# A decoder layer on one core: norm rows spread over the partitions by a store and a broadcast load instead of TensorE products, and the first head pair's key copies ahead of its value loads

## The chip, the core and the metric

The kernel runs on one core of a Trainium2 chip. The metric is the time of one execution in microseconds (us), smaller is better. Engines: PE (TensorE, matrix products), DVE (VectorE), ACT (ScalarE), POOL (GpSimd) and SP (SyncE, which here only issues DMAs). Each engine has its own instruction queue and works through it in order. A DMA is issued from an engine's queue; if what it moves isn't ready, the queue stands still at it, and everything behind it waits too.

## What is computed

One layer with 1024 tokens and 1024 features, all in float32. Cut to what matters here:

```python
def rmsnorm(x, g):
    return x * lax.rsqrt(jnp.mean(x * x, axis=-1, keepdims=True) + 1e-6) * g

h = x
h = h + 0.5 * rmsnorm(swiglu(rmsnorm(h, ffn1_pre_g), ...), ffn1_post_g)
h = h + rmsnorm(hybrid_mixer(rmsnorm(h, mix_pre_g), ...), mix_post_g)
h = h + rmsnorm(memory_cross_attention(rmsnorm(h, xa_pre_g), rmsnorm(mem, mem_g), ...), xa_post_g)
h = h + 0.5 * rmsnorm(swiglu(rmsnorm(h, ffn2_pre_g), ...), ffn2_post_g)
```

`hybrid_mixer` projects its input once, runs 16 heads of stick-breaking attention on one part and a state-space scan (SSD) on the other, norms the attention's output (1024 features) and the scan's (two groups of 512), and multiplies both by `w_out`. `mem` holds 256 tokens. So every stage begins and ends with a norm: one number for each token, by which all features of the token are multiplied.

## The kernel before

**Layout.** Activations lie transposed: a tile has 128 features on its partitions and 512 tokens along it, eight tiles make the 1024 features, and the tokens are done in two halves, called `hh` 0 and 1. Every operand of a large product is split into a high and a low part, and three matmuls stand for one (`mm3`): high by high, high by low, low by high. The weights are split on ACT (`whi`) and DVE (`wlo`) as they arrive, or earlier, and then written to DRAM ready split (`dwhi`, `dwlo`).

**A norm** takes two steps. `rms_cols` (L322) takes a tile in which the squares of all features have been added up, and multiplies each block of 128 tokens by ones on PE: this gives a column `c` with one partition for each token of a block and one column for each block (128 x 4 for a half, 128 x 8 for both, 128 x 2 for the memory). ACT takes the root and DVE the reciprocal. But the tiles to be scaled have the tokens along the row, and need the number of each token on all 128 partitions. This is what `rms_rows` (L346) makes: for each block PE multiplies the column, broadcast, by the identity into the PSUM tile `ms`, of which there is one, and ACT copies the 512 numbers into the row tile `r`. DVE then multiplies tiles by `r`. The columns are called `cpost` and `cpre` (behind and ahead of a stage), `cy` (the scan's two groups), `cmem` (the memory) and `ca` (the attention's output), and the rows `rpost`, `rpre`, `rm`, `mix_r` and `rn`. In all `rms_rows` is called 20 times.

**The stages**, by when they run in the profiled execution: the first feed-forward block's up-projection to about 545 us and down-projection to 658; the scan to 1010; the attention to 1541; the output projection to 1685; the cross-attention to 1928; the second feed-forward block to the end.

**What sets the order.** PE's order is the program's, but with pieces pinned: the kernel keeps a clock of the PE time that it has issued (`self.clock`, in ns), and `pinned(at)` puts a PE instruction where the clock says so. `self.later` holds steps with due times on the same clock (`post` fills it: columns, rows, then one tile after the other is scaled). `merge` runs two generators so that their PE time advances in a given proportion; the attention of pair `p` runs beside the projection of pair `p + 1`. On the other engines and in the DMA queues a scheduler orders what the program order leaves open.

**The attention's projection** (`inproj(p)`, L1655) makes queries, keys and values of two heads. `kevac` scales the keys by the norm row, splits them and copies them to their places with four DMAs from SP (L1700). The values are differenced, stored to DRAM (`vt`, L1727) and loaded back rearranged with four DMAs (`dv<-vt`, L1731), and `vtr` splits these. For pair 0 nothing runs beside the projection but its own steps. **The output projection** (`mix_out`) first adds up products over the scan's tiles, and then those over the attention's tiles in the PSUM tiles `dn`, of which there are four; each is scaled by the row `rn` made from `ca` as soon as `ca` is known, and only then is its place free.

Of the kernel before, what the change touches and what calls it, by code (L numbers as in the profile page):

```python
# [10 lines left out]
F32 = mybir.dt.float32  # L11
# [7 lines left out]
P = 128  # L19
# [6 lines left out]
MIXED = 6  # L26
# [21 lines left out]
class Kern:  # L48
# [270 lines left out]
                return e.value  # L319


    def rms_cols(self, groups, c, ones=None, r2=None):  # L322


        nc = self.nc
        ps = self.t(self.msp, [P, H], F32, "ms", bufs=1)
        nb = 0
        for g, accs in enumerate(groups):
            w = ones[g] if isinstance(ones, list) else self.ones if ones is None else ones
            for b in range(accs[0].shape[1] // P):  # L330
                for i, acc in enumerate(accs):
                    self.mm(
                        ps[:, nb : nb + 1], acc[:, b * P : (b + 1) * P], w, i == 0, i == len(accs) - 1
                    )
                nb += 1
        if r2 is not None:
            self.kp(nc.vector.tensor_tensor(out=c, in0=ps[:, 0:nb], in1=r2, op=ALU.mult))
            self.kp(nc.vector.tensor_tensor(out=c, in0=c, in1=r2, op=ALU.mult))
            self.kp(nc.scalar.activation(c, c, AF.Sqrt, bias=self.eps))
        else:  # L340
            self.kp(nc.scalar.activation(c, ps[:, 0:nb], AF.Sqrt, bias=self.eps))
        self.kp(nc.vector.reciprocal(c, c))
        if r2 is not None:
            self.kp(nc.vector.tensor_tensor(out=c, in0=c, in1=r2, op=ALU.mult))

    def rms_rows(self, c, r, behind=None):  # L346

# [35 lines left out]

        self.later += [(self.clock + start + step * d, lambda d=d: one(d)) for d in range(KT)]

    def post(self, hh, gname, r2, gnext=None, out=None, step=None, spread=True, pins=(23000, 28000), accs=None, at=None, tail=None, hold=False, late=None):


        nc = self.nc
        t1, t2 = 2500, 6000  # L390
        if accs is None:
            accs = self.new_accs()
# [2 lines left out]
        c = self.t(self.tp, [P, 4], F32, "cpost", bufs=2)  # L395
        r = self.t(self.fp, [P, H], F32, "rpost", bufs=1)

        def cols():
            self.rms_cols([accs], c, r2=r2)

        def rows():
            self.rms_rows(c, r)

        def apply(d):
            F = self.F[hh][d]
# [24 lines left out]
        accs2 = []  # L430
# [35 lines left out]
        if out is None:  # L466
            t -= 300
            c2 = self.t(self.rp, [P, 4], F32, f"cpre{hh}", bufs=2)
            r2_ = self.t(self.rp, [P, H], F32, f"rpre{hh}", bufs=1) if spread else None
            t1, t2 = tail or (t1 + 4000, t2 + 4000)  # L470
            self.held = [lambda: self.rms_cols([accs2], c2)]
# [9 lines left out]
        self.run_later(float("inf"))  # L481
        self.R[hh], self.C[hh] = self.next_norm

    def pre(self, hh, accs, t1, t2):
        c = self.t(self.rp, [P, 4], F32, f"cpre{hh}", bufs=2)
        r = self.t(self.rp, [P, H], F32, f"rpre{hh}", bufs=1)
        with self.pinned(t1):
            self.rms_cols([accs], c)
        with self.pinned(t2):
            self.rms_rows(c[:, :], r)  # L490
        self.R[hh], self.C[hh] = r, c


# [485 lines left out]
    def down1(self, sp, wdn, act_d, xs_d, gpost, gnext):  # L979

        place = self.blocks_down(sp)
        H_ = [[self.t(self.xp, [P, H], F32, f"xh{hh}{d}") for d in range(KT)] for hh in range(2)]
        L_ = [[self.xl(hh, F32) for d in range(KT)] for hh in range(2)]
        stay = {(1, 1): H_[0][4:8] + L_[0][4:8] + H_[0][0:3], (0, 0): H_[1][4:8] + L_[1][4:8] + H_[1][0:3]}
        accs = []

        def squares(hh, d, tag):
            if d == 0:
                accs[:] = self.new_accs(tag)
            self.sumsq(accs, d, self.F[hh][d])  # L990

        def at(t, f, *args):
            self.later.append((self.clock + t, lambda: f(*args)))

        def finish(m, i):
            if m == 3:
                self.run_later(float("inf"))
                for d in range(4):
                    at(5000 + 4000 * d, squares, 0, d, "acc0")
                self.resid(0, 3500, 16000)  # L1000
            elif m == 4:
                self.run_later(float("inf"))
# [247 lines left out]
    def ssd(self, close):  # L1250

        nc, ap = self.nc, self.ap
        with self.tc.tile_pool(name=self.nm("ssa"), bufs=1, reuse_waits="tile") as ep, \
# [269 lines left out]
                            nc.vector.tensor_tensor(out=yacc[hh], in0=yacc[hh], in1=sq, op=ALU.add)  # L1523

            def group_norm(gr):
                c = self.norm_c[gr] = self.t(self.rp, [P, 8], F32, f"cy{gr}")
                self.rms_cols([[y] for y in yacc], c, ones=self.ones512)
# [20 lines left out]
            def keys(n0, n1):  # L1548

                mh, ml, acc, rm = env["mem"]  # L1550
                if n0 == 0:
                    self.mem_c = self.t(self.rp, [P, 2], F32, "cmem")
                    self.rms_cols([[acc]], self.mem_c)
# [93 lines left out]
    def attention(self):  # L1647
        nc, ap = self.nc, self.ap
        with self.pools("at", ["o", "a"], ["w"]) as (op, sp, wsp, pp):
# [52 lines left out]
            def inproj(p):  # L1702
# [12 lines left out]
                def steps(hh, t, before):  # L1715
# [14 lines left out]
                    for q in range(4):  # L1730
                        nc.sync.dma_start(  # L1731
                            out=v[32 * q : 32 * q + 32, :].rearrange("e (j c d) -> e j c d", j=4, c=4), in_=rows[q]
                        )
                    return v

                def vtr(hh, t):

# [41 lines left out]
                for n in range(6):  # L1779
# [24 lines left out]

            def mix_row(i):
                self.mix_r.append(self.t(self.rp, [P, H], F32, f"rpre{i}", bufs=1))
                return self.rms_rows(self.norm_c[i][:, 0:4], self.mix_r[i], tr_tile)

            def scores(p, a, c):

# [106 lines left out]
            def memory_values(mh, ml):  # L1917

                rm = self.t(self.tp, [P, H], F32, "sq1")[:, 0:MEM]
                self.rms_rows(self.mem_c[:, :], rm)  # L1920
                yield
                for n in range(8):
                    w = ready.pop() if ready else next(Wm)
# [26 lines left out]
                yield from drain(0)  # L1950

            def beside():
                late.append(mix_row(1))
                self.first = self.mix_first(ready.pop())
                for n in range(4 * MIXED):
                    if n < 2:
                        for k in ((5, 6), (7,))[n]:
                            mix_split(k)
                    if n == 2:
                        late.pop()()  # L1960
# [10 lines left out]
            self.Wo, self.mix_r, ready, late = self.wstream(wo[0:MIXED]), [], [], []  # L1971
# [38 lines left out]
    def mix_out(self):  # L2010
# [3 lines left out]
        with self.pools("mo", ["r", "a"], ["b"]) as (rp, sp, sp2, dnp):  # L2014
# [53 lines left out]
            for n, (hh, part) in enumerate(passes):  # L2068
# [1 line left out]
                    continue  # L2070
                X = acts.pop(n)
                def norms(t):
                    c = self.norm_c[2] = self.t(self.rp, [P, 4], F32, "ca", bufs=2)
                    with self.pinned(self.clock + t):
                        self.rms_cols([asum[-1:]], c)
                    R[2] = norm_row(2, 0, t + 4000)

                if n == 1:
# [395 lines left out]
```

## Time and profile before

| | |
|---|---|
| time, median of 3 | 2585.72 us (2585.55 to 2587.47) |
| the profiled execution, its own time | 2583.27 us |
| its span | 2581.5 us |
| mean granted clock of PE | 0.999 |

By stages, from the profile's view by windows (us; the stages' limits are rounded):

| stage | from - to | PE busy | DVE busy | ACT busy | DMA share |
|---|---|---|---|---|---|
| feed-forward 1, up | 0 - 545 | 540.99 | 455.85 | 269.10 | 0.72 |
| feed-forward 1, down | 545 - 658 | 111.69 | 94.47 | 59.84 | 0.58 |
| scan | 658 - 1010 | 351.02 | 276.84 | 198.00 | 0.52 |
| attention | 1010 - 1541 | 526.49 | 406.85 | 295.40 | 0.64 |
| output projection | 1541 - 1685 | 144.00 | 110.70 | 63.70 | 0.60 |
| cross-attention | 1685 - 1928 | 242.98 | 157.86 | 136.16 | 0.62 |
| feed-forward 2 | 1928 - 2581.5 | 646.87 | 498.09 | 266.82 | 0.51 |

How to read the profile: a row of a timeline gives the start and the duration in us, the engine (SPq is SP's queue, which issues DMAs), the line of the kernel, the operation, output <- inputs and shape, and in brackets how long the engine was idle just before and what ended the idle time. `x4` at the end says that four like instructions are taken together. Matmuls overlap: what one costs is the distance between starts, not its duration. The view of waits says for PE which operation waited how long (total, times, longest) and for what. The view of DMAs gives for each kind the count, the KB of one and the median time from issue to landing.

### The profile page before, as it was taken

How to read it: one execution, taken by the hardware profiler on the slowest of the kernel's cores; microseconds unless marked ns; L12 is line 12 of the kernel's file. 1: busy time of each engine (PE TensorE's matmuls, PEld its weight loads, DVE VectorE, ACT ScalarE, POOL GpSimd, SP SyncE). 2: the span in 40 equal slices, each digit the busy share in tenths (PEclk: the TensorE clock that was granted, in tenths of full speed). 3: DMA queues.
4: the chain of work that ended last, by engine and by line, in shares of the span. 5: the costliest groups of instructions: out<-in, count | busy, mean ns of one | idle time of the engine just before them, and what ended most of it. 6: DMA issues, size and time to landing. Idle time of an engine off the chain costs nothing. (4 is left out here: it accounts for less than half of the span.)

```text
span 2581.5 us, 36855 instructions
## 1 busy us (share of the span) xinstructions
PE 2564.0 (99%) x12786; PEld 2141.0 (83%) x12786; DVE 2000.7 (78%) x3074; ACT 1289.0 (50%) x2302; POOL 576.5 (22%) x674
## 2 busy tenths in 40 slices
PE   9999999999999999999999999999999999999999
PEld 7888888888787778888888898888888888888887
DVE  7988997779689884787787876876656887777777
ACT  7434444555356663555555654455554433334453
POOL 2555553001000001111111110111012655541000
PEclk9999999999999999999999999999999999999999
DMA  6458988655665516666666655547658443327654
GB/s 240 163 180 293 308 290 305 220 185 166 232 205 197 184 72 212 186 177 160 176 171 152 206 167 202 197 155 260 202 185 304 150 162 111 110 82 237 192 175 147
DMA packets 251628, 498.24 MB, mean 193 GB/s; under 512 B 60592, under 2 KB 69168, under 8 KB 251440
## 3 DMA queue, kind: packets, MB, share of 16 engines
q1 hardware_dynamic: 204176, 387.31, 46.4%
q0 software_dynamic: 23360, 65.03, 8.6%
q10 hardware_dynamic: 23904, 43.53, 4.6%
q8 instruction: 101, 1.65, 0.3%
q14 instruction: 87, 0.71, 0.1%
HBM read 331.65 MB, written 143.13 MB: 184 GB/s over the span
## 5 line engine op out<-in xcount | busy, mean ns | idle before, releaser
L139 PE MATMUL mm<-xh,whi 128*128 128x512 f32 x1312 | 516.7, 403 | 1.1 <-DVE ft L668 0.5
L139 PE MATMUL mm<-xh,wlo 128*128 128x512 f32 x1280 | 491.7, 392 | 0.0
L139 PE MATMUL mm<-xl,whi 128*128 128x512 f32 (+1 forms) x1248 | 485.7, 389 | 0.3 <-DVE xl L277 0.3
L139 PEld LDWEIGHTS mm<-xh,wlo 128*128 128x128 f32 x1280 | 240.6, 188 | 52.4 <-DVE wlo L270 0.5
L139 PEld LDWEIGHTS mm<-xh,whi 128*128 128x128 f32 x1312 | 247.0, 188 | 43.1 <-issue 3.9
L139 PEld LDWEIGHTS mm<-xl,whi 128*128 128x128 f32 x1248 | 235.6, 189 | 33.4 <-DVE xl L277 0.8
L1829 DVE TENSOR_TENSOR_SCAN nb<-nb,begin 128x128 f32<-128x128 f32 (+7 forms) x128 | 172.1, 1347 | 32.3 <-ACT nb L1825 31.9
L1825 ACT ACTIVATE nb<-z,scale 128x128 f32<-128x128 f32 (+2 forms) x192 | 109.5, 580 | 89.5 <-PE z L139 88.6
L270 DVE TENSOR_TENSOR wlo<-wraw,whi 128x1024 fp32r<-128x1024 f32 x61 | 74.6, 1223 | 51.3 <-ACT whi L268 50.9
L268 ACT CAST whi<-wraw 128x1024 fp32r<-128x1024 f32 (+1 forms) x77 | 73.9, 959 | 70.4 <-PE mm L139 43.5
L1846 POOL DMA_DIRECT2D mix<-sq x64 | 53.0, 828 | 248.7 <-DVE sq L1844 181.5
L669 ACT ACTIVATE ft<-ft 128x512 f32<-128x512 f32 x88 | 55.5, 632 | 95.5 <-DVE ft L668 94.9
L139 PE MATMUL dn<-xh,wlo 128*128 128x512 f32 x296 | 101.2, 390 | 0.0
L772 POOL TENSOR_TENSOR wc<-raw,wraw 128x512 f32<-128x512 f32 x55 | 80.7, 1467 | 56.4 <-DVE wlo L270 23.4
L268 ACT CAST ath<-tr 128x512 fp32r<-128x512 f32 (+1 forms) x106 | 57.3, 540 | 66.9 <-PE tr L142 61.9
L772 POOL TENSOR_TENSOR wc<-wraw,raw 128x512 f32<-128x512 f32 x56 | 78.9, 1409 | 52.5 <-DVE whi L270 16.5
L871 POOL TENSOR_TENSOR ft<-ft,e 128x512 f32<-128x512 f32 x37 | 59.7, 1614 | 126.3 <-DVE e L867 51.1
L270 DVE TENSOR_TENSOR atl<-tr,ath 128x512 fp32r<-128x512 f32 (+1 forms) x106 | 66.1, 625 | 28.0 <-ACT ath L268 26.9
L139 PE MATMUL mm<-ath,v 128*128 128x256 f32 x320 | 87.8, 297 | 0.0
L139 PE MATMUL dn<-xh,blk 128*128 128x512 f32 x264 | 85.2, 389 | 0.0
L268 ACT CAST wlo<-wc 128x512 fp32r<-128x512 f32 x79 | 49.1, 621 | 69.2 <-PE dn L139 25.4
L139 PE MATMUL mm<-atl,v 128*128 128x256 f32 x320 | 83.1, 282 | 0.0
(601 smaller groups left out, 6795.2 us busy)
## 6 DMA issues: line engine op xcount, KB each, us to landing
whi<-dwhi SPq DMA_DIRECT2D x82, 512.0 KB, 4.1
wlo<-dwlo SPq DMA_DIRECT2D x82, 512.0 KB, 5.4
wraw<-in_w_gu SPq DMA_DIRECT2D x43, 512.0 KB, 4.0
dwhi<-bh SPq DMA_DIRECT2D x78, 256.0 KB, 4.2
dwlo<-bl SPq DMA_DIRECT2D x78, 256.0 KB, 4.2
raw<-in_w_gu SPq DMA_DIRECT2D x37, 512.0 KB, 4.1
wraw<-xs SPq DMA_DIRECT2D x56, 256.0 KB, 2.9
xs<-ft ACTq DMA_DIRECT2D x54, 256.0 KB, 3.0
```

The source lines that it names most:

```text
L139: self._pe(self.nc.tensor.matmul(out, lhsT, rhs, start=start, stop=stop, skip_group_check=self.more), cost)
L268: self.kp(self.nc.scalar.copy(hi, src))
L270: self.nc.vector.tensor_tensor(out=lo, in0=src, in1=hi.bitcast(F32), op=ALU.subtract)
L669: nc.scalar.activation(t, t, AF.Silu)
L772: inst = (nc.vector if early else nc.gpsimd).tensor_tensor(out=t, in0=a, in1=b, op=op)
L871: nc.gpsimd.tensor_tensor(out=t1, in0=t1, in1=e, op=ALU.mult)
L1825: nc.scalar.activation(nb[:, s0:s1], z[:, 0:n], AF.Sigmoid, scale=sc[:, i : i + 1])
L1829: nc.vector.tensor_tensor_scan(out=nb[:, 0:Wd][:, ::-1], data0=nb[:, 0:Wd][:, ::-1], data1=begin[:, S - Wd : S][:, ::-1], initial=0.0, op0 ...
L1846: nc.gpsimd.dma_start(out=self.mix_d[p][a * 64 : a * 64 + 64, csl], in_=o, accum_op=ALU.add)
```

## The change

`rms_cols` stores the finished column to DRAM, token by token in a row (`norm`), from SP's queue. The new function `row` loads that row back into all 128 partitions of the row tile with one broadcasting DMA, also from SP. 16 of the 20 calls of `rms_rows` become `row`. The four that stay on PE are the two that make the first rows of the kernel, the one behind the first feed-forward block's second half (`pe=True`), and the `cpre` row between the cross-attention and the second feed-forward block's second half. The columns `cy` and `cmem` are stored once and loaded several times.

In the attention the row `mix_r` is loaded earlier than it was computed. In pair 0, for the second half only, the four `dv<-vt` loads are issued behind the keys' copies, and `vtr` follows them.

```diff
-    def rms_cols(self, groups, c, ones=None, r2=None):
+    def rms_cols(self, groups, c, ones=None, r2=None, keep=True):
...
+        if keep:
+            kept = self.tc.dram_tile([nb, P], F32, name=self.nm("norm"))
+            nc.sync.dma_start(out=kept.rearrange("b p -> p b"), in_=c)
+            return kept
+
+    def row(self, kept, r):
+        self.nc.sync.dma_start(out=r, in_=kept.rearrange("b p -> (b p)").partition_broadcast(P))
...
 in post:
         def rows():
-            self.rms_rows(c, r)
+            if pe:
+                self.rms_rows(c, r)
+            else:
+                self.row(kept[0], r)
...
-                q.append((t + t2, lambda: self.rms_rows(c2[:, :], r2_)))
+                q.append((t + t2, lambda: self.row(kept[1], r2_)))
...
-        self.post(1, gpost, self.C[1], gnext, step=2000, accs=accs[:], at=(6500, 9000, 10000), tail=(7500, 10500))
+        self.post(1, gpost, self.C[1], gnext, step=2000, accs=accs[:], at=(6500, 9000, 10000), tail=(7500, 10500), pe=True)
...
 in the scan's keys and the attention's memory_values:
-                        self.rms_rows(self.mem_c[:, :], rm)
+                        self.row(self.mem_c, rm)
...
 in the attention's inproj, steps:
+                    def back():
+                        for q in range(4):
+                            nc.sync.dma_start(... in_=rows[q])
+                        return v
+                    return back if hh and p == 0 else back()
...
-                vtr(1, tv[1])
+                if p:
+                    vtr(1, tv[1])
                 kevac(evac((yield from last), 1), h1)
+                if p == 0:
+                    vtr(1, tv[1]())
...
-                if n == 10:
-                    late.append(mix_row(0))
-                if n == 12:
-                    late.pop()()
+                if n == 8:
+                    mix_row(0)
...
 in mix_out:
-                with self.pinned(self.clock + at):
-                    self.rms_rows(self.norm_c[i][:, 4 * hh : 4 * hh + 4], r)
+                if i < 2:
+                    self.row(self.norm_c[i][4 * hh : 4 * hh + 4], r)
+                else:
+                    with self.pinned(self.clock + at):
+                        self.row(self.norm_c[i], r)
```

**SP, the first pair's second half in the attention.** `vt` is the values' tile in DRAM, `dv` its rearranged copy, `k` the keys of the two heads, `xl` the split keys; `whi` and `wlo` are weights for later products. Before:

```order
L1717 DMA mix_130<-ev_10050 128x512
L1727 DMA vt_10057<-dv_10053 128x512
L182 DMA whi_10117<-dwhi_647 128x1024
L1700 DMA k_9855<-xl_2197_9851 64x512
L1731 DMA dv_10059<-vt_10057 32x16x32 x4
L1700 DMA k_9855<-xl_2198_9852 64x512
L1700 DMA k_9856<-xl_2197_9851 64x512
L1700 DMA k_9856<-xl_2198_9852 64x512
L182 DMA wlo_10118<-dwlo_648 128x1024
```

And in the changed kernel:

```order
L1732 DMA mix_130<-ev_10044 128x512
L1742 DMA vt_10051<-dv_10047 128x512
L182 DMA whi_10111<-dwhi_647 128x1024
L1715 DMA k_9849<-xl_2199_9845 64x512
L1715 DMA k_9849<-xl_2200_9846 64x512
L1715 DMA k_9850<-xl_2199_9845 64x512
L1715 DMA k_9850<-xl_2200_9846 64x512
L1748 DMA dv_10053<-vt_10051 32x16x32 x4
L182 DMA wlo_10112<-dwlo_648 128x1024
```

The four loads of the values' rows stood between the first and the second copy of the keys, and now stand behind the fourth.

**SP, the beginning of the output projection's sums over the attention.** `xl` are activations loaded from `h`, `slo` the scan's tiles, `wraw` weights that are yet to be split. Before:

```order
L382 DMA xl_3532_16186<-h_1270_5772 128x512
L382 DMA xl_3538_16227<-h_1271_5773 128x512
L2041 DMA slo_16256<-mix_138 128x512
L2041 DMA slo_16261<-mix_139 128x512
L185 DMA wraw_16265<-in_w_out 128x1024
L185 DMA wraw_16271<-in_w_out 128x1024
L382 DMA xl_3552_16284<-h_1272_5774 128x512
```

And in the changed kernel, where `norm_16201` is the column `ca` in DRAM and `rn_3536` the row that scales the `dn` tiles:

```order
L352 DMA rn_3591_16499<-norm_9094 128x512
L352 DMA rn_3592_16501<-norm_9796 128x512
L185 DMA wraw_16243<-in_w_out 128x1024
L185 DMA wraw_16249<-in_w_out 128x1024
L185 DMA wraw_16329<-in_w_out 128x1024
L347 DMA norm_16201<-ca_16193 128x4x1
L185 DMA wraw_16335<-in_w_out 128x1024
L352 DMA rn_3536_16203<-norm_16201 128x512
L390 DMA xl_3537_16205<-h_1271_5773 128x512
L2059 DMA slo_16234<-mix_138 128x512
L2059 DMA slo_16239<-mix_139 128x512
```

Four weight loads in a row come ahead of the activations, the column's store stands between the third and the fourth of them, and the row's load directly behind the fourth, ahead of the activations' loads.

**DVE at the same place.** `sq<-dn,rn` is the first `dn` tile scaled by the row. Before:

```order
L342 RECIPROCAL ca_16212<-ca_16212 128x4
L270 TENSOR_TENSOR wlo_16274<-wraw_16271,whi_16273 128x1024
L2007 TENSOR_TENSOR sq_3539_16234<-dn_16177,rn_3536_16220 128x512
L2008 TENSOR_TENSOR xl_3254_14922<-xl_3254_14922,sq_3539_16234 128x512
L2007 TENSOR_TENSOR sq_3540_16250<-dn_16192,rn_3536_16220 128x512
```

In the changed kernel:

```order
L342 RECIPROCAL ca_16193<-ca_16193 128x4
L270 TENSOR_TENSOR wlo_16252<-wraw_16249,whi_16251 128x1024
L270 TENSOR_TENSOR wlo_16332<-wraw_16329,whi_16331 128x1024
L2025 TENSOR_TENSOR sq_3538_16212<-dn_16158,rn_3536_16203 128x512
L2026 TENSOR_TENSOR xl_3255_14912<-xl_3255_14912,sq_3538_16212 128x512
```

A second weight split now stands between the reciprocal and the first scaling.

More of the change, by code (lines that the diff above doesn't have):

```diff
@@ L384, in resid, with post @@
         self.later += [(self.clock + start + step * d, lambda d=d: one(d)) for d in range(KT)]
-    def post(self, hh, gname, r2, gnext=None, out=None, step=None, spread=True, pins=(23000, 28000), accs=None, at=None, tail=None, hold=False, late=None):
+    def post(self, hh, gname, r2, gnext=None, out=None, step=None, spread=True, pins=(23000, 28000), accs=None, at=None, tail=None, hold=False, late=None, pe=False):
         nc = self.nc
@@ L396, in post @@
         r = self.t(self.fp, [P, H], F32, "rpost", bufs=1)
+        kept = []
         def cols():
-            self.rms_cols([accs], c, r2=r2)
+            kept.append(self.rms_cols([accs], c, r2=r2, keep=not pe))
         def rows():
-            self.rms_rows(c, r)
+            if pe:
+                self.rms_rows(c, r)
+            else:
+                self.row(kept[0], r)
         def apply(d):
@@ L470, in post @@
             t1, t2 = tail or (t1 + 4000, t2 + 4000)
-            self.held = [lambda: self.rms_cols([accs2], c2)]
+            self.held = [lambda: kept.append(self.rms_cols([accs2], c2, keep=spread))]
             if not hold:
@@ L482, in flush, with pre @@
         self.R[hh], self.C[hh] = self.next_norm
-    def pre(self, hh, accs, t1, t2):
+    def pre(self, hh, accs, t1, t2, pe=True):
         c = self.t(self.rp, [P, 4], F32, f"cpre{hh}", bufs=2)
@@ L487, in pre @@
         with self.pinned(t1):
-            self.rms_cols([accs], c)
+            kept = self.rms_cols([accs], c, keep=not pe)
         with self.pinned(t2):
-            self.rms_rows(c[:, :], r)
+            if pe:
+                self.rms_rows(c[:, :], r)
+            else:
+                self.row(kept, r)
         self.R[hh], self.C[hh] = r, c
@@ L1525, in group_norm @@
             def group_norm(gr):
-                c = self.norm_c[gr] = self.t(self.rp, [P, 8], F32, f"cy{gr}")
-                self.rms_cols([[y] for y in yacc], c, ones=self.ones512)
+                c = self.t(self.rp, [P, 8], F32, f"cy{gr}")
+                self.norm_c[gr] = self.rms_cols([[y] for y in yacc], c, ones=self.ones512)
             def mem_prep():
@@ L1551, in keys @@
                 if n0 == 0:
-                    self.mem_c = self.t(self.rp, [P, 2], F32, "cmem")
-                    self.rms_cols([[acc]], self.mem_c)
+                    self.mem_c = self.rms_cols([[acc]], self.t(self.rp, [P, 2], F32, "cmem"))
                     yield
@@ L1729, in steps @@
                     rows = o.rearrange("(c e) (j q d) -> q e j c d", c=4, q=4, d=32)
[L1730 to L1734, printed above, removed]
+                    def back():
+                        for q in range(4):
+                            nc.sync.dma_start(
+                                out=v[32 * q : 32 * q + 32, :].rearrange("e (j c d) -> e j c d", j=4, c=4), in_=rows[q]
+                            )
+                        return v
+                    return back if hh and p == 0 else back()
                 def vtr(hh, t):
@@ L1806, in mix_row @@
                 self.mix_r.append(self.t(self.rp, [P, H], F32, f"rpre{i}", bufs=1))
-                return self.rms_rows(self.norm_c[i][:, 0:4], self.mix_r[i], tr_tile)
+                self.row(self.norm_c[i][0:4], self.mix_r[i])
             def scores(p, a, c):
@@ L1919, in memory_values @@
                 rm = self.t(self.tp, [P, H], F32, "sq1")[:, 0:MEM]
-                self.rms_rows(self.mem_c[:, :], rm)
+                self.row(self.mem_c, rm)
                 yield
@@ L1952, in beside @@
             def beside():
-                late.append(mix_row(1))
+                mix_row(1)
                 self.first = self.mix_first(ready.pop())
@@ L1958, in beside @@
                             mix_split(k)
-                    if n == 2:
-                        late.pop()()
                     if 4 <= n < 11:
@@ L1970, in attention @@
             wo = [self.wsrc("out", 8 * part + d) for n in range(2) for part in (1, 0) for d in range(8)]
-            self.Wo, self.mix_r, ready, late = self.wstream(wo[0:MIXED]), [], [], []
+            self.Wo, self.mix_r, ready = self.wstream(wo[0:MIXED]), [], []
             for p in range(7):
@@ L2059, in norm_row @@
                 r = self.t(rp, [P, H], F32, f"rn{i}")
-                with self.pinned(self.clock + at):
-                    self.rms_rows(self.norm_c[i][:, 4 * hh : 4 * hh + 4], r)
+                if i < 2:
+                    self.row(self.norm_c[i][4 * hh : 4 * hh + 4], r)
+                else:
+                    with self.pinned(self.clock + at):
+                        self.row(self.norm_c[i], r)
                 return r
@@ L2072, in norms @@
                 def norms(t):
-                    c = self.norm_c[2] = self.t(self.rp, [P, 4], F32, "ca", bufs=2)
+                    c = self.t(self.rp, [P, 4], F32, "ca", bufs=2)
                     with self.pinned(self.clock + t):
-                        self.rms_cols([asum[-1:]], c)
+                        self.norm_c[2] = self.rms_cols([asum[-1:]], c)
                     R[2] = norm_row(2, 0, t + 4000)
```

## The prediction

> **What bounds the kernel now.** I read the page first, for which engine has no slack.
>
> ```profile
> span 2581.5 us, 36855 instructions
> PE 2564.0 (99%) x12786; PEld 2141.0 (83%) x12786; DVE 2000.7 (78%) x3074; ACT 1289.0 (50%) x2302; POOL 576.5 (22%) x674
> ```
>
> PE is busy for 2564.0 of 2581.5 us. Work taken off PE shortens the kernel one for one as long as nothing else then becomes late, and only 17.5 us of waiting are there to be won besides. Next I asked the view of waits for PE; its two largest rows are these (waits in us: total, times, longest).
>
> ```profile
> PE z L139 <- DMA k<-xl: 1.9, 1, 1.9
> PE ms L139 <- DVE atl L270: 1.9, 1, 1.9
> ```
>
> Both lie where the change works: the first is the wait for the first pair's keys, the second stands ahead of a norm product on PE.
>
> **The products that go.** The listing of instructions shows 20 spreading products before and 4 after: 14 with four blocks and 2 with two blocks (the memory's norm) are removed. The page's busy time per group overlaps its neighbours, so I price one by start times, in the timeline of PE at the last one (start, duration).
>
> ```profile
> 1930.14 0.39 PE L139 MATMUL mm<-xh,whi 128*128 128x512 f32 x1
> 1930.36 1.05 PE L139 MATMUL ms<-ident,cpost 128*128 128x128 f32 x8
> 1931.17 0.48 PE L139 MATMUL mm<-xl,whi 128*128 128x512 f32 x1
> 1931.49 0.39 PE L139 MATMUL mm<-xh,wlo 128*128 128x512 f32 x1
> 1931.72 0.39 PE L139 MATMUL mm<-xh,whi 128*128 128x512 f32 x1
> ```
>
> The product holds PE from 1930.36 to 1931.17, 0.81 us, and the matmul behind it takes 0.32 us to the next start where the others take 0.23: another 0.09. That is 0.90 us each, 14 x 0.90 = 12.6 us. The two-block product is in the timeline too:
>
> ```profile
> 971.70 0.61 PE L139 MATMUL ms<-ident,cmem 128*128 128x128 f32 x4
> 972.06 0.36 PE L139 MATMUL mm<-xs,whi 128*128 128x256 f32 x1
> 972.26 0.28 PE L139 MATMUL mm<-u,whi 128*128 128x256 f32 x1
> ```
>
> 0.36 us plus a late neighbour (0.20 to the next start) makes about 0.45, twice 0.9. **Sum of the products: 13.5 us**, nearly evenly spread over the kernel. The 16 PSUM copies on ACT go as well; ACT is at 50% and I count nothing for them.
>
> The second memory product has the 1.9 us wait ahead of it: it needs the one "ms" bank, which DVE is still reading.
>
> ```profile
> 1497.82 0.49 PE L142 MATMUL ms<-ident,nb 128*128 128x128 f32 x3
> 1500.18 0.71 PE L139 MATMUL ms<-ident,cmem 128*128 128x128 f32 x4 [1.87 <-DVE atl L270]
> 1500.00:1502.00 2.00, 1.82 (x15) 1.00 0.00 0
> ```
>
> The last row is from the view by windows (length, PE busy, granted clock, DMA share, GB/s); the clock stays at 1.00. What PE does next is a product whose transposes were made several steps earlier, so the wait goes with its cause: **1.9 us**. It is bounded by 0 (the next transpose to the bank waits instead) and 1.9; I take 1.9.
>
> **The first pair's keys.** PE's and SP's timelines, and PE's clock in two windows behind the wait:
>
> ```profile
> 1035.63 0.34 PE L139 MATMUL z<-k,wraw 128*128 128x384 f32 x1
> 1037.90 0.36 PE L139 MATMUL z<-k,q 128*128 128x256 f32 x1 [1.93 <-DMA k<-xl]
> 1038.25 0.63 PE L139 MATMUL mm<-xh,whi 128*128 128x512 f32 x1
> 1038.68 0.63 PE L139 MATMUL mm<-xl,whi 128*128 128x512 f32 x1
> 1041.45 0.39 PE L139 MATMUL z<-k,q 128*128 128x384 f32 x1
> ...
> 1038.00:1040.00 2.00, 2.00 (x7) 0.53 0.98 271
> 1040.00:1042.00 2.00, 2.00 (x9) 0.61 0.75 195
> ```
>
> ```profile
> 1032.02 0.50 SPq L1700 DMA_DIRECT2D k<-xl  x1
> 1032.62 2.63 SPq L1731 DMA_DIRECT2D dv<-vt  x4
> 1035.35 1.86 SPq L1700 DMA_DIRECT2D k<-xl  x3
> ```
>
> PE waits 1.93 us, and then runs at a granted clock of 0.53 and 0.61: a 512-column matmul takes 0.43 us (1038.25 to 1038.68) instead of 0.23 until about 1041.45. Of those 3.2 us, 3.2 x (1 - 0.23/0.43) = 1.5 are lost. On SP the four loads of the values' rows stand between the first and the second copy of the keys and cost 2.7 us of issue. Now the second copy follows at about 1032.75, when DVE has its operand, and lands after the 2.55 us that the last rows give (1035.35 to 1037.90): 1035.3, ahead of 1035.97, when PE asks. **3.4 us go.** The displaced loads start some 2 us later; their casts are moved back on ACT and DVE, and the values' upper half is read only by the third query block, so nothing is charged; uncovered, it would be a wait of the same size, 3.4 us. In the Trainium skill, "TensorE: Matmul & The Clock Gate", section "Part 1: The HAM clock gate", the clock falls after an idle window of about 3.4 us that runs freely. The trace agrees only in part: 1.93 us of idling were enough here and 1.87 us at 1498 were not. By an unconditional 3.4 us the clock would not have fallen and the keys would be worth 1.9, the sum 17.3.
>
> **What is added: a store, a wait, a broadcast load.** Thirteen stores and 16 loads more go through SP: a store is 128 x 4 words, each of 4 bytes to a place of its own; the load behind it, of 256 KB, waits on SP until the store has landed (the gated and the memory's norms are stored long before their six loads). No row shows a store in 4-byte pieces. The nearest rows, of the view of DMAs (KB each, us to landing), the first with pieces of 128 bytes, the second the plain store of the same tiles, and the loads behind a weight load at the tightest place:
>
> ```profile
> vt<-dv SPq DMA_DIRECT2D x16, 256.0 KB, 2.6
> dv<-vt SPq DMA_DIRECT2D x64, 64.0 KB, 2.6
> ...
> xl<-h SPq DMA_DIRECT2D x2, 256.0 KB, 4.2
> slo<-mix SPq DMA_DIRECT2D x2, 256.0 KB, 5.0
> ```
>
> 512 pieces of 128 bytes land no later than whole rows. I take 2.6 us for the store (bounds 2.6 and, doubled for smaller pieces, 5.2) and 4.2 to 5.0 for the load: 7 to 8 us where PE and ACT needed 2. The tightest place is the attention group's norm in the output projection. DVE, then PE, then SP:
>
> ```profile
> 1561.65 0.18 DVE L342 RECIPROCAL ca<-ca 128x4 f32<-128x4 f32 x1 [0.69 <-ACT ca L341]
> 1562.59 1.23 DVE L270 TENSOR_TENSOR wlo<-wraw,whi 128x1024 fp32r<-128x1024 f32 x1 [0.76 <-ACT whi L268]
> 1566.35 0.69 DVE L2007 TENSOR_TENSOR sq<-dn,rn 128x512 f32<-128x512 f32 x1 [2.54 <-ACT rn L355]
> ...
> 1549.18 0.39 PE L139 MATMUL dn<-ohi,whi 128*128 128x512 f32 x1
> 1572.83 0.39 PE L139 MATMUL dn<-ohi,whi 128*128 128x512 f32 x1
> ...
> 1559.66 4.51 SPq L185 DMA_DIRECT2D wraw<-in_w_out  x2
> 1564.22 0.90 SPq L382 DMA_DIRECT2D xl<-h  x2
> ```
>
> Four "dn" banks of 24 matmuls are filled from 1549.18 on; the fifth starts at 1572.83 (0.90 earlier without the product: 1571.9) and needs the first one scaled by the row. The store can go out at 1561.9, lands at 1564.5; SP has by then issued the next weight load, which waits for DVE's split that ends at 1563.8; the row lands at 1568.8 to 1569.6. DVE now has one more weight split ahead of the scaling, which ends near 1568.8. The scaling may start as late as 1571.1, so 1.5 to 2.3 us are spare with the store at 2.6 and about nothing with 5.2. Behind the waiting load stand ten loads of activations and the last weight load, which PE uses only at about 1589. The second half repeats the hand-over with as much room.
>
> The other norms have more cover. At the last one, on DVE:
>
> ```profile
> 1932.07 1.42 DVE L407 SCALAR_TENSOR_TENSOR F<-F,params,rpost 128x512 f32<-128x512 f32 x2 [1.73 <-ACT rpost L355]
> 1958.70 0.69 DVE L910 TENSOR_TENSOR ft<-ft,mm 128x512 f32<-128x512 f32 x1 [2.93 <-PE mm L139]
> 1965.07 0.69 DVE L668 TENSOR_TENSOR ft<-mm,rpre 128x512 f32<-128x512 f32 x1 [5.59 <-PE mm L139]
> ```
>
> The norm's work starts some 2 us later, queueing the gates' scalings behind it, and DVE still has 2.93 and 5.59 us idle before the second half begins; without that cover the 2 us would reach PE. I charge 1 us in all for waits I can't see. **The sum:** 13.5 + 1.9 + 3.4 - 1 = 17.8, rounded 18. The profiled execution took 2583.27 us (span 2581.5 and 1.8 around it), 2.45 under the median of the three runs, 2585.72; on it the result is 2565.3, on the median 2567.7.
>
> **Rivals.**
> *The gain is partly given back by a new order.* PE's order in attention's last pair changes, since the merging is by PE time, and the transposes change banks. DVE is at 78%, so a wait for a split can appear; the 0.3 to 1.9 us waits there now speak for it. Two to four such waits of 2 us leave 10 to 14 us: 2572 to 2576. The same holds if the keys' wait becomes one for the values.
> *The round trip is late by a little.* With 5 to 6 us for the store both hand-overs in the output projection stall by 1 to 2 us, perhaps with 1.5 us of low clock each: 2 to 7 us back, 2570 to 2575.
> *Slower.* The same place, if the 4-byte store takes far longer. Every microsecond past the slack comes twice. 18.8 - 2 x 1.5 leaves 15.8, half of it 7.9: from a landing time of some 12 us (2.6 + 1.9 + 7.9) the gain is gone, at 15 us the time is about 2592. Against it: pieces of 128 bytes cost nothing visible. The Trainium skill speaks for it: "DMA: Bandwidth & Descriptors", section "Rules for kernel authors", says that a non-contiguous last dim lowers to one descriptor per element, and "Specifications" that under 512 bytes a read-modify-write is done. It gives no price for that; no run here shows one.
> *The change doesn't do what it says:* DVE or the loads already bound PE just behind its queue, so that freed PE time turns into waiting. Then only waits that vanish count, 0 to 5 us: 2581 to 2586. PE's few waits speak against it.
>
> **How the numbers follow.** Forecast 62% (2564 to 2571), new order 20%, slightly late trip 10%, no effect 4%, slower 4%. The range reaches from 2563 (a gain of 22 to 23, if small waits go too) to 2578, which takes in the first two rivals. A change under 0.2%, 5.2 us, can't be told from none: faster 0.91, same 0.05, slower 0.04.
>
> **What would show it.** PE should have four products left, busy time lower by about 12 us or more (overlaps aside), no wait for k and none for atl ahead of the memory's values, and a clock of 1.00 at 1038. The store's time to landing should be near 2.6 us and the rows' 4 to 5. DVE should scale the first "dn" bank in the output projection before PE's fifth bank starts. A wait of PE for a "dn" bank there, or in the view of waits a new row of several us, makes the prediction wrong.

## The result, and the profile after

The changed kernel is slower: 2660.47 us (median of 4, 2654.99 to 2664.09) against 2585.64 us in the same series, a ratio of 1.029 (95% interval 1.0271 to 1.031). The forecast was 2567.7. The page of the changed kernel, the lines that answer to the first two quoted of before:

```profile
span 2653.2 us, 36638 instructions
PE 2575.2 (97%) x12666; PEld 2139.5 (81%) x12666; DVE 1999.5 (75%) x3074; ACT 1280.9 (48%) x2286; POOL 577.1 (22%) x674
```

PE has 120 matmuls fewer and yet is busy for 11.2 us more, since its clock falls behind long waits (behind one of 5.2 us it was 0.50 from 629 to 633 us); and it is idle for 78.0 us (2653.2 - 2575.2) where it was for 17.5. The 71.7 us of span are 60.5 of idling and 11.2 of busy time. As some 13.5 us of products are gone (the prediction's sum), the slower running must have cost some 25; that is an estimate. Whom PE waits for, in the view of waits (us: total, times, longest):

```profile
PE dn L139 <- DVE sq L2025: 7.8, 2, 4.6
PE ms L139 <- DVE cpost L344: 7.1, 1, 7.1
PE dn L139 <- ACT pt L268: 7.0, 1, 7.0
PE mm L139 <- DMA wlo<-dwlo: 6.7, 4, 2.2
PE ms L139 <- DVE acc L377: 6.2, 2, 6.0
PE mm L139 <- DVE dg L1576: 5.6, 1, 5.6
```

And DVE, in the same view:

```profile
DVE F L420 <- DMA rpost<-norm: 28.6, 3, 13.3
DVE u L1275 <- DMA rpre<-norm: 22.5, 2, 12.1
DVE sq L2025 <- DMA rn<-norm: 12.7, 2, 7.0
DVE dg L1576 <- DMA Ct<-norm: 6.2, 1, 6.2
```

The wait for the keys and the one ahead of the memory's values are gone. In their place stand waits of 4 to 7 us spread over the kernel, and DVE stands 70 us for rows. The view of DMAs gives the reason (KB each, median us from issue to landing):

```profile
rpost<-norm SPq DMA_DIRECT2D x5, 256.0 KB, 5.5
norm<-cpost SPq DMA_DIRECT2D x5, 2.0 KB, 10.0
norm<-cpre SPq DMA_DIRECT2D x3, 2.0 KB, 9.0
norm<-cy SPq DMA_DIRECT2D x2, 4.0 KB, 13.1
norm<-ca SPq DMA_DIRECT2D x2, 2.0 KB, 9.9
norm<-cmem SPq DMA_DIRECT2D x1, 1.0 KB, 8.1
```

A store of 2 KB takes 9 to 10 us (medians), where the 256 KB row takes 5.5. And it isn't slow alone. SP's timeline at the first such store (start, duration):

```profile
605.77 0.37 SPq L347 DMA_DIRECT2D norm<-cpost  x1
606.20 0.50 SPq L1071 DMA_DIRECT2D wraw<-xs  x1
...
614.25 0.32 SPq L352 DMA_DIRECT2D rpost<-norm  x1
```

The view of DMAs for the 1.8 us from 606.1 on, with the rate in 40 slices, and the landings of what was issued there:

```profile
GB/s 364 364 364 410 501 273 364 319 501 319 364 455 319 273 183 274 48 140 51 52 52 7 50 2 47 1 46 46 1 46 46 91 0 46 0 46 91 0 137 46
...
wraw<-xs SPq DMA_DIRECT2D x1, 256.0 KB, 11.1
raw<-in_w_dn SPq DMA_DIRECT2D x1, 256.0 KB, 11.0
raw<-xs SPq DMA_DIRECT2D x1, 256.0 KB, 11.3
norm<-cpost SPq DMA_DIRECT2D x1, 2.0 KB, 8.4
```

Here the core's transfers fall from over 300 GB/s to about 46 (mean of the last 24 slices), and from 608 to 616 us they stay at 27 to 49 in windows of 2 us. The three large loads issued behind the store take 11 us. In the kernel before, the loads at this place took 3.0 to 3.8; two of them:

```profile
raw<-in_w_dn SPq DMA_DIRECT2D x1, 256.0 KB, 3.0
wraw<-xs SPq DMA_DIRECT2D x1, 256.0 KB, 3.8
```

At the next store DVE runs dry, as the view by windows shows (length, busy time of each engine, clock, DMA share, GB/s). The low rate there is no measure of the hold-up, since SP stands at the row's load, and the loads issued before the store have landed by 670.7 us:

```profile
667.00:675.00 8.00, 8.00 (x41) 6.77 (x40) 1.55 (x5) 0.63 (x2) 0.00 (x0) 1.00 0.12 34
```

What follows there is one chain; SP, then DVE, then PE:

```profile
667.52 0.38 SPq L347 DMA_DIRECT2D norm<-cpre  x1
675.41 0.33 SPq L352 DMA_DIRECT2D rpre<-norm  x1
...
681.07 0.69 DVE L1275 TENSOR_TENSOR u<-mm,rpre 128x512 f32<-128x512 f32 x1 [10.42 <-DMA rpre<-norm]
...
682.91 2.04 PE L139 MATMUL ms<-ident,cpost 128*128 128x128 f32 x8 [7.13 <-DVE cpost L344]
```

From the column to the row it takes 13.5 us. DVE stands at the first multiplication that needs the row, and the next norm's column, queued behind it on DVE, keeps PE waiting 7.13 us.

To see where the time goes, the starts of the same matmuls can be compared. The table gives how many us later than in the profiled execution of before PE is at nine points of the program (named by the time in before), for this kernel and for the experiments below. A single execution differs from another by up to 4 us up to 600 us, where nothing is changed, so a difference of 1 or 2 us between two points can be chance.

```
at (us)               600   700   985  1030  1065  1545  1690  1925  end
changed kernel        0.0  14.7  28.0  28.0  30.9  27.8  42.3  59.5  71.7
rows_from_pool        0.6  19.8  38.7  38.8  46.2  43.2  65.3  85.6 101.5
pieces_behind_stall   0.3  20.3  34.0  34.0  38.3  35.2  52.2  67.7  78.1
stores_only           1.1   6.5   6.5  10.0  13.9  14.0  18.1  24.3  24.7
stores64             -0.6  -0.4  -0.4  -0.4  -1.6  -1.8  -1.8  -1.9  -1.1
pieces128             3.3   6.5   6.8   6.9   5.3   2.3  -1.7   0.7   1.4
keys_only             4.2   4.0   3.9   3.9   3.0   2.7   2.7   2.6   2.9
far_only             -0.1   0.0   1.7   7.3  10.6   7.4   5.3   5.3   5.8
far128               -0.5  -0.8   0.8   0.8  -0.3  -3.4  -5.5  -5.5  -5.9
mix128               -1.0  -1.2  -1.1  -1.1  -2.7  -5.8  -8.7  -9.3  -9.7
mix128_ffn1           1.4   4.4   4.4   4.4   3.4   0.3  -2.4  -3.1  -2.9
```

The changed kernel loses wherever a store has just been made, and gains 3 us in the attention (1065 to 1545), where rows are loaded from stores made long before and the wait ahead of the memory's values is gone.

### The profile page after: what moved, and what is told of

It is laid out like the page before. It is cut to its first block, busy times and chain, and to the rows that moved or that the text cites. A ratio compares the mean times of both kernels' runs of the same rounds, so it can differ in the third digit from the quotient of the medians.

```text
span 2653.2 us, 36638 instructions
## 1 busy us (share of the span) xinstructions
PE 2575.2 (97%) x12666; PEld 2139.5 (81%) x12666; DVE 1999.5 (75%) x3074; ACT 1280.9 (48%) x2286; POOL 577.1 (22%) x674
## 5 line engine op out<-in xcount | busy, mean ns | idle before, releaser
L139 PE MATMUL dn<-xh,whi 128*128 128x512 f32 x240 | 82.8, 390 | 0.7 <-DMA whi<-dwhi 0.7
```

The costliest lines, as they stand in the source:

```text
L139: self._pe(self.nc.tensor.matmul(out, lhsT, rhs, start=start, stop=stop, skip_group_check=self.more), cost)
```

## The experiments

Each is timed against the kernel before on the same chip (2584.6 to 2585.2 us there); n is the number of runs.

**probe_stores.** Four kinds of store added to the kernel before:

```diff
+        if nb == 4:            # one of the four, in turn
+            nc.sync.dma_start(out=pa.rearrange("b p -> p b"), in_=c)     # (a): pa [nb, P]
+            nc.sync.dma_start(out=pb, in_=c)                             # (b): pb [P, nb]
+            nc.sync.dma_start(out=pc[:, :, 0], in_=c)                    # (c): pc [P, nb, 16]
+            nc.sync.dma_start(out=pd, in_=self.ident[0:nb, :])           # (d): pd [nb, P]
```

> The kernel before, and behind each norm column of four blocks one store to DRAM that nothing reads, in turn of four kinds: (a) as in the change, 512 pieces of 4 bytes side by side; (b) the column as it lies, 128 pieces of 16 bytes; (c) 512 pieces of 4 bytes, each 64 bytes from the next; (d) 4 rows of 512 bytes (from another tile). Theory S (small pieces land late): (a) 8 to 11 us as in the changed kernel, (b) and (c) in between, (d) 2 to 3 us. Rival G (any store lands late in this traffic): all four kinds 8 us or more. The time is that of before within 0.3%, since nothing waits for these stores.

2588.95 us (one run). The view of DMAs, where pa, pb, pc are kinds (a), (b), (c); a group without a last number has no landing on record:

```profile
pb<-cpre SPq DMA_DIRECT2D x4, 2.0 KB, 4.2
pc<-cpost SPq DMA_DIRECT2D x3, 2.0 KB, 3.0
...
pa<-cpre SPq DMA_DIRECT2D x1, 2.0 KB, 9.0
...
pa<-ca SPq DMA_DIRECT2D x1, 2.0 KB, 10.6
```

Rival G, that any store lands late in this traffic, is out. But theory S in its plain form is out too: (c) moves as many pieces of 4 bytes as (a), and lands in 3.0 us. Small pieces are not slow here; small pieces side by side are. For (d) nothing was learnt: its stores had nothing to wait for, went out at the start, and no landing of theirs is on record.

**rows_from_pool.** `row` issues from `nc.gpsimd` instead of `nc.sync`.

> The changed kernel, but the rows' loads are issued from POOL's queue, so that SP isn't held up while a store is under way. Theory S (the row comes late to DVE, because the store lands late): the stores land as late as before, DVE still waits 10 us and more for rows, and the time stays within 10 us of the changed kernel, 2650 to 2670. Rival Q (the load that waits on SP holds the weights' loads back, and this is the loss): most of the 75 us is back, 2570 to 2600.

2677.4 us (n = 4), 1.036 (1.0345 to 1.0376): 17 us slower still than the changed kernel. SP no longer stands at a row's load in its queue, and DVE waits for rows as before and more:

```profile
DVE F L420 <- DMA rpost<-norm: 32.1, 4, 15.4
DVE u L1275 <- DMA rpre<-norm: 29.9, 2, 15.0
```

So it is not SP's queue that costs the time. The expected bound of 2670 was missed: POOL's queue is a worse place for these loads, which wasn't followed further.

**pieces128.** The column is transposed on DVE, and four DMAs store it in pieces of 128 bytes:

```diff
-            nc.sync.dma_start(out=kept.rearrange("b p -> p b"), in_=c)
+            self.kp(nc.vector.tensor_copy(self.wide[:, 0:nb], c))
+            self.kp(nc.vector.transpose(self.turned, self.wide))
+            for q in range(4):
+                nc.sync.dma_start(out=kept[:, 32 * q : 32 * q + 32], in_=self.turned[32 * q : 32 * q + nb, :])
```

> The changed kernel, but the column is first transposed in blocks of 32 by 32 on DVE and stored with four DMAs in pieces of 128 bytes (16 pieces in place of 512); the rows' loads and all the rest as in the change. Theory S: the stores land in 2.5 to 3.5 us instead of 8 to 13, the row is there about 8 us behind the column, and most of the loss goes: 2568 to 2590. If 2568 is reached, the prediction's other terms were right. Rival Q or G: the stores' size doesn't matter, 2640 or more.

2584.84 us (n = 10), 1.0001 (0.9992 to 1.001). All of the 75 us is back, though the rows go the same way. Of the forecast gain of 18 us nothing is there. On SP the row's load now goes out 3.7 us behind the store's first DMA (8.5 in the changed kernel), but DVE still waits for rows, most of all where the scan begins. SP's and DVE's timelines:

```profile
610.79 1.35 SPq L350 DMA_DIRECT2D norm<-place  x4
...
614.48 0.32 SPq L355 DMA_DIRECT2D rpost<-norm  x1
...
674.39 0.69 DVE L1278 TENSOR_TENSOR u<-mm,rpre 128x512 f32<-128x512 f32 x1 [6.97 <-DMA rpre<-norm]
```

The table shows where it wins and loses: 3.2 us lost from 600 to 700, 2.4 from 1690 to 1925; 3.0 won from 1065 to 1545 and 4.0 from there to 1690.

**stores_only and stores64.** The kernel before, its rows all made by PE, with the change's 13 stores added and read by nobody; in the second the pieces are 64 bytes apart:

```diff
+        if keep:
+            kept = self.tc.dram_tile([nb, P], F32, name=self.nm("norm"))
+            nc.sync.dma_start(out=kept.rearrange("b p -> p b"), in_=c)
 stores64:
+            kept = self.tc.dram_tile([nb, P, 16], F32, name=self.nm("norm"))
+            nc.sync.dma_start(out=kept[:, :, 0].rearrange("b p -> p b"), in_=c)
```

> The kernel before (all rows still made by PE), with the change's 13 stores added at the same places, 512 neighbouring pieces of 4 bytes, read by nobody. Theory H (such a store holds up all transfers of the core for 8 to 10 us): weights and activations come late although no row waits for a store, 2610 to 2650, with transfers of 10 us and more behind each store. Theory L (only the row's own late arrival costs): 2585 to 2591.

> As stores_only, the same number and size of pieces from the same places, but each piece 64 bytes from the next in DRAM. If it is neighbours within the same 64 bytes that are slow: stores land in 2.5 to 3.5 us, the transfers behind them aren't held up, 2585 to 2590. If it is the number of small pieces: the same as stores_only.

stores_only: 2606.6 us (n = 4), 1.0073 (1.0055 to 1.009), a loss of about 20 us by stores that nothing waits for, somewhat under what was expected. stores64: 2584.95 us (n = 10), 1.0002 (0.9993 to 1.0011). stores_only's view of DMAs, first for the 1.9 us behind its first store, then for all its stores behind `cpost`:

```profile
wraw<-xs SPq DMA_DIRECT2D x1, 256.0 KB, 10.7
raw<-in_w_dn SPq DMA_DIRECT2D x1, 256.0 KB, 10.5
...
norm<-cpost SPq DMA_DIRECT2D x5, 2.0 KB, 9.4
```

And the same view of stores64:

```profile
norm<-cpost SPq DMA_DIRECT2D x5, 2.0 KB, 3.1
norm<-cpre SPq DMA_DIRECT2D x3, 2.0 KB, 2.6
```

It is the same behind the other stores. Of the transfers issued within 2 us behind one, from SP's queue and from POOL's, those with a landing on record took 8.5 to 16.2 us in stores_only (18 of them, median 10.9), and 2.9 to 6.9 in stores64 (19, median 4.5). Theory H is shown: neighbouring 4-byte pieces hold up the core's other transfers, and with a gap the same pieces cost nothing.

**keys_only.** The kernel before with the four `dv<-vt` loads and `vtr` moved behind the keys, as in the change.

> The kernel before with only the first pair's keys put ahead of the values' loads, and the values' split behind the keys' one. The prediction's term: 3.4 us less, 2582. By what the other runs show of this place (their lag against before falls by 2.4 us there): 2583. A new wait in place of the old one: 2585 or more.

2586.19 us (n = 11), 1.0002 (0.9993 to 1.0011): a gain of 3.4 us is excluded. The wait for the keys is gone, and PE's waits from 1030 to 1110 us have a new row:

```profile
PE mm L139 <- DMA wlo<-dwlo: 1.6, 1, 1.6
```

That is one weight's low half, which SP issues at 1058.21 and which lands at 1064.81. SP's timeline, and PE's behind it:

```profile
1038.58 3.49 SPq L1733 DMA_DIRECT2D dv<-vt  x4
1042.17 0.56 SPq L182 DMA_DIRECT2D wlo<-dwlo  x1
...
1057.57 0.59 SPq L182 DMA_DIRECT2D whi<-dwhi  x1
1058.21 0.45 SPq L182 DMA_DIRECT2D wlo<-dwlo  x1
...
1064.86 0.50 PE L139 MATMUL mm<-xh,wlo 128*128 128x512 f32 x1 [1.65 <-DMA wlo<-dwlo]
```

In the kernel before, the same weight's two halves, by their number in the queue, went out at 1041.68 and 1042.22, ahead of the queries' copies; now it goes out 16 us later, behind them. The order on SP changed beyond the four loads that were moved; why it did so is not shown.

In the table the lag falls by 0.9 us from 1030 to 1065 here, and by 1.1 to 1.6 in pieces128, far128 and mix128. That is no proof of a gain, since it falls by 1.2 in stores64 too, where the keys are as before. There PE waits at the same product, and yet the clock behind it stays at 1.00. The view puts this wait down to the values' split, which ends within 0.1 us of the keys' landing at 1037.7. The view of waits, then a window (length, PE busy, clock, DMA share, GB/s):

```profile
PE z L139 <- ACT v L268: 2.2, 1, 2.2
1038.00:1040.00 2.00, 2.00 (x11) 1.00 0.93 289
```

probe_gaps shows the same: a wait of 2.0 us there, and a clock of 1.00 behind it. So the low clock that the prediction read behind this wait doesn't come with it in every execution.

**far_only, far128.** Rows by DMA only from stores made long before (`cy` four times, `cmem` the second time), the keys ahead, all other rows on PE. far128 differs in the stores' form alone, as in pieces128.

> Of the change only what has time: the rows of the scan's two groups (four loads) and the memory's second row come by DMA from stores made long before, the first pair's keys go ahead of the values; all other rows stay on PE. All theories: from before go 4 x 0.90 + 0.45 us of products, the 1.9 us wait ahead of the memory's values, and 3.4 us at the keys: 9.3 us, 2576. If the keys' move gives nothing: 2580. If rows by DMA cost by themselves wherever they are: 2586 or more.

> far_only with its three stores in pieces of 128 bytes instead of 4 and nothing else changed. If three stores of neighbouring 4-byte pieces cost far_only the 10 us that its lag grows by from 990 to 1045 us: 2577 to 2580. If that loss has another cause: 2586 or more.

far_only: 2588.64 us (n = 11), 1.0011 (1.0 to 1.0021). far128: 2577.36 us (n = 8), 0.9976 (0.9965 to 0.9986). Three stores of neighbouring 4-byte pieces, none of them waited for soon, cost some 9 to 11 us (by the ratios and by the medians). The row by DMA is not dear where it has time.

**mix128, mix128_ffn1.** far128 with DMA rows also in the output projection (`ca` twice, and its two closing norms); then three more in the first feed-forward block.

> The stores in 128-byte pieces; rows by DMA only where there is time: the scan's groups (four), the memory's second use, the attention's norm in the output projection (two) and that stage's two closing norms; all others on PE as before; the keys' copies ahead. Of products go 8 x 0.90 + 0.45 = 7.65 us, the wait ahead of the memory's values 1.9 and 2.4 us at the keys: 12 us, 2573. If the rows' way of 8 us costs in the output projection too: 2578 to 2585.

> mix128, and in the first feed-forward block three more rows by DMA (the closing norm of the first half, and the two opening norms of the scan), stored in 128-byte pieces. By products it would gain 3 x 0.90 = 2.7 us on mix128: 2573. If a round trip of some 8 us is late at this place even when no transfer is held up (in pieces128 the lag grows by 5 us from 640 to 700 us): 2579 to 2583.

mix128: 2575.98 us (n = 5), 0.9964 (0.9952 to 0.9977), faster than both kernels of the case. mix128_ffn1: 2580.35 us (n = 11), 0.9984 (0.9975 to 0.9992): three products fewer, and 4.4 us slower. From 600 to 700 it loses 3.0 us where mix128 gains 0.2.

**probe_gaps.** The first probe again, with the 4-byte pieces 8, 16, 32 or 64 bytes apart.

> The kernel before, and behind each norm column of four blocks one store of 512 pieces of 4 bytes that nothing reads, the pieces in turn 8, 16, 32 and 64 bytes apart. If the writes to one 64-byte stretch of DRAM hold each other up: the landing falls with the gap, from near 9 us (4 bytes apart) over 5 to 7 us at 8 and 16 bytes to about 3 us at 64. If only pieces that touch each other are slow: about 3 us for all four gaps.

2585.34 us (one run). Four stores of each kind landed in 3.0 to 8.4 us at 8 bytes, 2.3 to 6.7 at 16, 2.0 to 3.3 at 32 and 2.8 to 6.3 at 64. Neither expectation is met cleanly: most of the slowness is gone as soon as the pieces don't touch, yet two of the four at 8 bytes took 5.5 and 8.4. How wide the stretch is within which pieces hold each other up stays open.

**pieces_behind_stall.** pieces128 with the change's 4-byte store, unread, ahead of each of its own.

> pieces128, and ahead of each of its 13 stores in 128-byte pieces the change's store of the same column in neighbouring 4-byte pieces, to a place that nothing reads. No row waits for a 4-byte store here. If the 4-byte store holds up all transfers behind it, the 128-byte pieces and the rows too: as slow as the changed kernel within 15 us, 2645 to 2670, with the same waits of DVE for rows. If the row only suffers by the landing of the store that it waits for: the 21 us of stores_only on top of pieces128, 2600 to 2612.

2660.84 us (n = 4), 1.0297 (1.028 to 1.0314), the changed kernel's time. No row waits for a 4-byte store here, and yet the first row's load goes out 11.1 us behind the first DMA of its own store, where it was 3.7 in pieces128. DVE waits for rows about as long as in the changed kernel:

```profile
DVE u L1280 <- DMA rpre<-norm: 27.0, 2, 13.8
DVE F L425 <- DMA rpost<-norm: 22.2, 4, 8.3
DVE sq L2030 <- DMA rn<-norm: 13.2, 2, 7.2
```

So the hold-up of the transfers is the cause of the 75 us. About 20 come by what it does to weights and activations (stores_only). The other 55 are a difference: that they come from the rows' own two transfers standing in it fits this run, but they were not measured by themselves.

## Why the prediction was wrong

**The step that failed** is "I take 2.6 us for the store (bounds 2.6 and, doubled for smaller pieces, 5.2)". The stores took 7.9 to 13.1. The rows under it were misread. The prediction takes `vt<-dv` for a store in pieces of 128 bytes and `dv<-vt` for the plain store; but `vt<-dv` is the plain store, of whole rows, and `dv<-vt` is a load, in 512 pieces of 128 bytes. So neither row shows a store in small pieces, and the price came from a load. What matters is where the pieces go: 512 pieces of 4 bytes, 64 bytes apart, land in about 3 us, and side by side in 9 to 10. That the stores with gaps come near the 2.6 is luck. Doubling the row was no upper bound. The sign that the prediction named for being wrong came too: a wait of PE for a `dn` bank is the first row of its waits in the changed kernel (7.8 us).

**A second step failed with it.** The rival that ended slower was this mechanism, but it had 4 in 100, and was priced only as a landing time at one place, the output projection, with a break-even at 12 us. The landing times were 8 to 13, and the loss 75 us, because close hand-overs paid all over the kernel and because the store held up transfers that have nothing to do with it. The sum had no term for that. The Trainium skill, "DMA: Bandwidth & Descriptors", section "Specifications", which the prediction weighed there, has a read-modify-write under 512 bytes. stores64, with 4-byte pieces throughout and no loss, shows that the size by itself doesn't price such a store; whether the pieces that touch wait for each other's read-modify-write, no run here shows.

**"I charge 1 us in all for waits I can't see"** was too small, even with a quick store. pieces128 is the kernel that the prediction had in mind, and its gain is 0 (-0.1% to +0.08%), not 18. Three rows in the first feed-forward block, which save 2.7 us of products, lose 4.4 us net (mix128_ffn1 against mix128); the "more cover" that the prediction gave to all other norms was read at the last norm only.

**"3.4 us go" at the keys** failed too: the timing of keys_only shows no gain (1.8 us at the most, by its interval). Of the 3.4, 1.5 were the low clock, which other executions with the same wait don't have (stores64, probe_gaps). The wait of 1.9 went, but a weight that SP now issues 16 us later brought one of 1.6, at a place where the prediction counted nothing. The 17.3 that the prediction names for the case without the low clock leaves out its own charge of 1 us; its terms make 16.3.

**What held.** The products are worth about what was said where the row has time. far128 saves four rows of 0.90, one of 0.45 and the 1.9 us ahead of the memory's values: 6.0 in all; 7.2 were measured (2584.56 - 2577.36; by the interval 3.6 to 9.0). mix128 saves four more rows, 3.6, so 9.6 in all; 9.0 were measured (2584.96 - 2575.98; 5.9 to 12.4). In the output projection, the place that the prediction called tightest, mix128 shows no wait of PE for a scaled `dn` bank, as had been worked out for a store of 2.6 us. Its five products gone there are worth 4.5, and 2.9 are won from 1545 to 1690: PE waits 1.7 us for a weight's split on DVE.

## What to carry to other kernels

A DMA that writes neighbouring words one at a time is priced neither by its bytes nor by its own landing time: here it held up the other transfers, so look at the landings behind it, and turn the tile first so that the pieces are long (here 128 bytes, two short DVE instructions). A value sent through DRAM takes some 7 to 8 us (in pieces128 from 667.0, when the column is turned, to 674.4, when DVE has the row) and pays only where the consumer is further away than that; with DMA rows only where there is such time and the near rows left on PE, the same idea gains 0.36%. When a wait is removed by moving transfers, look at what the queue issues later in its new order.

## What was not expected of the hardware

512 neighbouring 4-byte writes, 2 KB in all, held the core's transfers at 27 to 49 GB/s for 8 us at the first store of the changed kernel, where over 300 had been moved. Loads of 256 KB behind them took 11 us instead of 3 to 4, and not in SP's queue alone: in far_only a store from POOL's queue, issued 0.8 us behind such a store of 1024 pieces, took 16.3 us to land (its kind takes 4.8 in the kernel before). Even the store of 256 pieces (1 KB) took 8.1 us; one of 1024 (4 KB) took 13.1. By which mechanism touching pieces hold up the rest stays open.

The same wait of PE isn't always followed by a low clock: behind 1.9 us of idling it was 0.53 and 0.61 in the kernel before, and behind 2.2 us at the same product 1.00 in stores64.
